# Block sums moved from VectorE to GpSimd in a one-core decoder layer

## The chip, the cores and the metric
The kernel runs on one core of a Trainium2 chip. The metric is the time of one execution on the device in microseconds (us). The kernel before took 449.89 us, the median of 3 runs (449.35 to 450.27).

The core has a matrix engine (TensorE, PE in the profile, with its weight loads as PEld), a vector engine (VectorE, DVE), an activation engine (ScalarE, ACT), a general engine (GpSimd, POOL), and SyncE (SP), which issues the transfers. Each works through a queue of its own in order and waits on semaphores for the others. SBUF is the working memory of all of them; PSUM receives what the matrix engine sums.

## The reference, cut to what matters
One decoder layer over 256 tokens of width 1024. The input is normalised and multiplied by one wide weight, whose columns feed a recurrent branch, a causal attention, a cross-attention over 256 memory tokens, and three gates. A gated sum of the three branches goes through an output projection, and a gated feed-forward block of width 3072 follows. All of it is float32.

```python
h = rms_norm(x, mix_norm_gain[l])
proj = h @ w_in[l]
xa, ga, qm, km, vm, qx, g_logits = jnp.split(proj, splits, axis=-1)
...
branch_out = jnp.einsum("bsnw,nwd->bsnd", ys, w_branch[l])
gates = jax.nn.sigmoid(g_logits)          # three gates, 1024 columns each
merged = jnp.sum(gates * branch_out, axis=2)
x = x + merged @ w_out[l]
...
x = x + (jax.nn.gelu(g) * (h @ w_ffn_up[l])) @ w_ffn_down[l]
```

## The kernel before
**Precision.** Every operand of a product is split in two: ScalarE copies it to a rounded high part, VectorE subtracts that from the operand and keeps the low part. A product is three matmuls: high by high, high by low, low by high.

**Weights.** They arrive in units of 128 x 2048 elements (1 MB). `dma_next` (L138) loads a unit into one of three `wraw` buffers, `split_next` (L173) makes `whi` on ScalarE (L189) and `wlo` on VectorE (L190), three buffers each, and `ahead` (L205), called after each unit's matmuls, keeps the loads four units and the splits two units ahead.

**The first gate as seven products.** The first gate's weight, 1024 rows by 1024 columns, is not multiplied as four plain blocks. It is cut in 2 x 2 blocks B11, B12, B21, B22, and x in 2 x 2 blocks too (two halves of the tokens, two halves of the columns). Four sums S1 to S4 of the blocks of x (L715 to L728) and four sums T1 to T4 of the blocks of the weight stand in for the missing eighth product, in the manner of Strassen and Winograd; `product` (L779) multiplies one block of 128 tokens x 512 by one of 512 x 512, in 12 matmuls.

**Sums of x.** L718 adds the high and low parts of the normalised x again into two tiles `xg` of 128 x 1024. L721 to L724 make S1 and S2 (in `sa`) and S3 and S4 (in `sb`), 128 x 512 each. L727 and L728 split `sa` and `sb` into `sh` and `sl`, two slots at a time.

**Sums of weights.** `add2` (L153) adds two units half by half, 128 x 1024 each. `block_t1` (L157) loads B12 into two tiles and writes T1 = B11 + B12 over B11's buffer, once B11 is split. `block_t2` (L164) loads B22 into the buffer with the tag `sc`, which the cross-attention's probabilities `px` used before, then writes T3 = B12 + B22 over B12, and T2 = T1 + B22 into two new tiles. T4 = T2 + B21 goes over T2 (L182). Their order of use is T2, T1, T3, T4.

**Order of work.** The text is traced in its written order; a scheduler then orders each engine's queue, and lets a later instruction go ahead where an earlier one would still wait by its estimate. The tiles named `s4`, among them `xg`, `sa`, `sb`, B12, and the operands of the cross-attention, share 15 buffers of 128 x 1024. Around the change the written order is: scores of the last heads of the cross-attention (`x_qk`), softmax (`x_norm`, L663), the first half of the third gate's unit with the split of B11 and T1 behind it, transposes of the probabilities and their splits (`x_pt`, L671 to L674), the sums of x, the products with the values (`x_pv`, L682 to L684), the second half of the third gate, then the first block product, branch 1, and the block product of S2 with T2 (L800 to L804).

Of the kernel before, what the change touches and what calls it, by code (L numbers as in the profile page):

```python
# [8 lines left out]
F32 = mybir.dt.float32  # L9
F32R = mybir.dt.float32r  # L10
AF = mybir.ActivationFunctionType
OP = mybir.AluOpType
# [95 lines left out]
def hybrid_trunk(ctx: ExitStack, tc: tile.TileContext, ws, xw, xv, xn, mt, mn, pp, lw, fg, out):  # L108
    nc = tc.nc
    V, A, T, G = nc.vector, nc.scalar, nc.tensor, nc.gpsimd  # L110
# [16 lines left out]
    def a8(nm):  # L127
        t = a8p.tile([128, KC, S], F32R, name=nm, tag="a8")
        return t
# [4 lines left out]
    raw, hi, lo = {}, {}, {}  # L134
# [12 lines left out]
    blk = {}  # L147
    HW = UW // 2

    def halves(t):  # L150
        return [t[:, :HW], t[:, HW:]]

    def add2(o, a, b):  # L153
        for x, y, z in zip(o, a, b):
            V.tensor_add(x, y, z)

    def block_t1(b11):  # L157
        blk["B12"] = [s4("b12", sh=(128, HW)) for _ in range(2)]
        for t, c in zip(blk["B12"], (0, HW)):
            nc.sync.dma_start(t, ws[NU - 2, :, c:c + HW])  # L160
        blk["T1"] = halves(raw[b11])
        add2(blk["T1"], blk["T1"], blk["B12"])

    def block_t2():  # L164
        b22 = ip.tile([128, UW], F32, name="b22", tag="sc", bufs=1)
        nc.sync.dma_start(b22, ws[NU - 1])
        blk["B22"] = halves(b22)
        blk["T3"] = blk["B12"]
        add2(blk["T3"], blk["B12"], blk["B22"])
        blk["T2"] = [s4("t2", sh=(128, HW)) for _ in range(2)]  # L170
        add2(blk["T2"], blk["T1"], blk["B22"])

    def split_next(parts=1):  # L173
        i = st["spl"]
        u = STEPS[i]
        h = wp.tile([128, UW], F32R, name="whi")
        l = wp.tile([128, UW], F32R, name="wlo")
        if u == "T2":
            block_t2()
        elif u == "T4":  # L180
            blk["T4"] = blk["T2"]
            add2(blk["T4"], blk["T2"], halves(raw[i0["B21"]]))  # L182
        if isinstance(u, str):
            src = list(zip(blk[u], halves(h), halves(l)))
        else:
            w = UW // parts
            src = [[t[:, p * w:(p + 1) * w] for t in (raw[u], h, l)] for p in range(parts)]
        for r, hh, ll in src:
            A.copy(hh, r)  # L189
            V.tensor_sub(ll, r, hh.bitcast(F32))  # L190
        hi[i], lo[i] = h, l
        if u == i0["B11"]:
            block_t1(u)
        st["spl"] += 1

    T2S = STEPS.index("T2")
    i0 = {"B11": STEPS[T2S - 2], "B21": STEPS[STEPS.index("B22") - 2]}
# [7 lines left out]
    def ahead():  # L205
        u = st["u"] - 1
        n = max(x for x in STEPS[:min(u + LA_D, NS - 1) + 1] if not isinstance(x, str))
        while st["dma"] <= n:
            dma_next()
        while st["spl"] <= min(u + LA_S, NS - 1):  # L210
            split_next()
# [75 lines left out]
    for k in range(KC):  # L287
        t = ip.tile([128, 1024], F32, name="xw", tag="s4", bufs=15)
# [24 lines left out]
    def s4(nm, dt=F32, sh=(128, 4, S)):  # L313
        t = ip.tile(list(sh), dt, name=nm, tag="s4", bufs=15)
        return t
# [13 lines left out]
    xh, xl = a8("xh"), a8("xl")  # L329
# [3 lines left out]
    for k in range(KC):  # L333
# [7 lines left out]
        else:  # L341
            A.activation(xh[:, k, :], xk, AF.Copy, scale=par("g1", k))
        V.scalar_tensor_tensor(xl[:, k, :], xk, par("g1", k), xh[:, k, :].bitcast(F32),
                               op0=OP.mult, op1=OP.subtract)
# [3 lines left out]
        for j, (a, b) in enumerate(((h, xh), (h, xl), (l, xh))):  # L348
            for m in range(4):
                c = slice(512 * (k % 4) + m * 128, 512 * (k % 4) + m * 128 + 128)  # L350
                T.matmul(b0[m][:, :S], lhsT=a[:, c], rhs=b[:, k, :], start=(k == 0 and j == 0),  # L351
                         stop=(k == KC - 1 and j == 2))
    st["spl"] = st["u"] = 2
    split_next(2)
    split_next(2)
    ahead()
    sq = s4("sq", sh=(128, D))
# [47 lines left out]
    e, z, y, q, n8 = [cst.tile([128, 4], F32, name=f"sp{i}") for i in range(5)]  # L405
# [271 lines left out]
    def x_pv(h):  # L677
        b = ac_bank()
        for m in range(2):
            hs_ = slice(h * 128, (h + 1) * 128)  # L680
            ph, pl = pxs[h]
            mm3(b[:, :S], mvh[:, m, hs_], mvl[:, m, hs_], ph[:, m, :], pl[:, m, :], m == 0, m == 1)  # L682
        A.copy(ych[:, h, :], b[:, :S])
        V.tensor_sub(ycl[:, h, :], b[:, :S], ych[:, h, :].bitcast(F32))  # L684
# [6 lines left out]
    for g in range(2):  # L691
        d = slice(2 * g, 2 * g + 2)
# [9 lines left out]
    for t in range(2):  # L702
        A.activation(mvh[:, t, :], vb[t], AF.Copy, scale=rsm[:, t:t + 1])
        V.scalar_tensor_tensor(mvl[:, t, :], vb[t], rsm[:, t:t + 1], mvh[:, t, :].bitcast(F32),
                               op0=OP.mult, op1=OP.subtract)
# [8 lines left out]
    sh, sl = a8p.tile([128, 4, 4, 128], F32R, name="sh", tag="a8"), a8p.tile([128, 4, 4, 128], F32R, name="sl", tag="a8")  # L714
    xg = [s4("xg"), s4("xg")]  # L715
    for kh in range(2):
        k = slice(4 * kh, 4 * kh + 4)
        V.tensor_add(xg[kh], xh[:, k, :].bitcast(F32), xl[:, k, :].bitcast(F32))  # L718
    a11, a21, a12, a22 = [xg[i][:, :, t * 128:(t + 1) * 128] for i in range(2) for t in range(2)]
    sa, sb = s4("sa", sh=(128, 2, 4, 128)), s4("sb", sh=(128, 2, 4, 128))  # L720
    V.tensor_sub(sa[:, 0], a22, a21)  # L721
    V.scalar_tensor_tensor(sa[:, 1], a11, -1.0, sa[:, 0], op0=OP.mult, op1=OP.subtract)
    V.tensor_sub(sb[:, 0], a11, a21)
    V.scalar_tensor_tensor(sb[:, 1], a12, -1.0, sa[:, 1], op0=OP.mult, op1=OP.subtract)  # L724
    for i, t in ((0, sa), (1, sb)):
        d = slice(2 * i, 2 * i + 2)
        A.copy(sh[:, d], t)  # L727
        V.tensor_sub(sl[:, d], t, sh[:, d].bitcast(F32))  # L728
    x_pv(0)
    x_pv(1)  # L730
    x_pt(3)
# [118 lines left out]
    for i in range(2):  # L850
        t = a8p.tile([128, 4, 2, S], F32R, name="h2", tag="a8")
# [73 lines left out]
    def ffn_gate(f, bk):  # L925
        g = gp[f % 3]
        t = fp.tile([128, 2, S], F32, name="tcv", bufs=3)
        t2 = join(bk)
        V.tensor_mul(g[:, :, 2:], t2, rb2x)
        for m in range(2):  # L930
            b = 2 * f + m
            A.activation(t[:, m, :], g[:, m, 2:], AF.Identity, scale=par("fw", 48 + b), bias=par("fb", b))
            V.scalar_tensor_tensor(t[:, m, :], g[:, m, 1:1 + S], par("fw", 24 + b), t[:, m, :], op0=OP.mult, op1=OP.add)
            V.scalar_tensor_tensor(t[:, m, :], g[:, m, 0:S], par("fw", b), t[:, m, :], op0=OP.mult, op1=OP.add)  # L934
        A.activation(t, t, AF.Gelu_apprx_tanh)  # L935
        return t
# [45 lines left out]
    for f in range(1, 13):  # L982
        if f < 12:
# [4 lines left out]
            t = ffn_gate(f, gbk)  # L988
# [14 lines left out]
    for i, (t, c0, c1) in enumerate(FIN):  # L1003
        o = dz[i - 3][:, :256] if i > 2 else db[t][c0 // 512][:, c0 % 512:c0 % 512 + c1 - c0]
        V.scalar_tensor_tensor(yf[:, t, c0:c1], o, rs2[:, t:t + 1], (yf if i > 2 else x2)[:, t, c0:c1], op0=OP.mult,
                               op1=OP.add)
        x = slice(t, t + 1)
# [20 lines left out]
        for c in (512, 768):  # L1028
            V.scalar_tensor_tensor(yg[:, t, c:c + 256], yf[:, t, c:c + 256], r3[:, x], fgb[:, c:c + 256], op0=OP.mult,
                                   op1=OP.mult)  # L1030
# [75 lines left out]
```

## Time and profile before
| | us | share of the span |
|---|---|---|
| profiled execution, device time | 449.81 | |
| its span | 448.0 | 100% |
| PE, 2486 matmuls | 438.4 | 98% |
| PEld | 383.2 | 86% |
| DVE, 458 instructions | 345.5 | 77% |
| ACT, 374 instructions | 274.9 | 61% |
| POOL, 21 instructions | 18.9 | 4% |

Busy time is time in which an engine had an instruction running; the ends of matmuls are modelled and they overlap, so that the step from one start to the next tells more than a duration. A row of the timeline gives the start, the time, the engine, the line of the code, the operation, output and inputs with their shapes, the count of merged instructions, and in brackets the idle time before it with what ended that. PEclk is the matrix engine's granted clock as a share of 2.4 GHz.

### The profile page before, as it was taken

The numbers are of one execution on the slowest core, as the hardware profiler recorded it, in microseconds if no ns is written. First come the engines' busy times: TensorE is split into PE (matmuls) and PEld (weight loads), VectorE is DVE, ScalarE is ACT, GpSimd is POOL, SyncE is SP. The second block draws the span as 40 slices with busy tenths as digits, with TensorE's granted clock in tenths as the row PEclk, the third lists the DMA queues.
The fourth block names the chain that finished last, engine by engine and source line by source line (L and its number), as shares of the span: only waits on it lengthen the run. The fifth ranks groups of instructions, "written<-read, shape, count | busy, mean of one in ns | idle before, by whom it ended". The sixth has DMA issues, their size and how long they took to land.

```text
span 448.0 us, 6270 instructions
## 1 busy us (share of the span) xinstructions
PE 438.4 (98%) x2486; PEld 383.2 (86%) x2486; DVE 345.5 (77%) x458; ACT 274.9 (61%) x374; POOL 18.9 (4%) x21
## 2 busy tenths in 40 slices
PE   9999999999999899999999999999999999999994
PEld 9999879998888688888888888888888888888883
DVE  6679799999699997848767798766676677677664
ACT  6675989986655547554347676554554554554543
POOL 2000200130000000000001200000000000000011
PEclk9999999999999899999999999999999999999999
DMA  8975753556525356265445555545545555545102
GB/s 300 412 283 189 282 197 140 189 191 223 191 93 189 98 192 274 94 228 201 168 169 199 199 203 189 189 181 190 195 178 200 196 178 208 193 162 222 53 0 94
DMA packets 13852, 84.38 MB, mean 188 GB/s; under 512 B 1792, under 2 KB 2304, under 8 KB 4608
## 3 DMA queue, kind: packets, MB, share of 16 engines
q1 hardware_dynamic: 13392, 82.95, 50.3%
q0 software_dynamic: 144, 0.52, 0.5%
q10 hardware_dynamic: 288, 0.52, 0.3%
q8 instruction: 19, 0.31, 0.3%
q14 instruction: 9, 0.07, 0.0%
HBM read 82.94 MB, written 1.05 MB: 187 GB/s over the span
## 4 chain that ended last, share of the span: by engine, by line
PE 91%; DVE 6%; ACT 1%; issue 1%; DVEq 0%; ACTq 0%
PE mm L234 18%; PE mm L237 9%; PE ac L976 5%; PE ac L977 5%; PE ac L978 5%; PE ac L247 4%; PE ac L248 4%; PE ac L249 4%; PE mm L785 4%; PE mm L247 3%; PE mm L248 3%; PE mm L249 3%; PE mm L219 3%; PE mm L220 3%; PE mm L221 3%; PE mm L351 3%
## 5 line engine op out<-in xcount | busy, mean ns | idle before, releaser
L190 DVE TENSOR_TENSOR wlo<-wraw,whi 128x2048 fp32r<-128x2048 f32 (+1 forms) x74 | 164.1, 2220 | 68.8 <-ACT whi L189 68.5
L189 ACT CAST whi<-wraw 128x2048 fp32r<-128x2048 f32 (+1 forms) x74 | 135.9, 1839 | 79.4 <-PE mm L234 29.8
L234 PE MATMUL mm<-h,whi 128*128 128x512 f32 x352 | 88.8, 392 | 0.0
L234 PEld LDWEIGHTS mm<-h,whi 128*128 128x128 f32 x352 | 63.7, 189 | 11.6
L237 PEld LDWEIGHTS mm<-h,wlo 128*128 128x128 f32 x352 | 48.6, 190 | 3.8
L237 PE MATMUL mm<-h,wlo 128*128 128x256 f32 x352 | 49.7, 282 | 0.0
L976 PE MATMUL ac<-whi,ah 128*128 128x512 f32 x92 | 35.9, 392 | 0.0
L977 PE MATMUL ac<-wlo,ah 128*128 128x512 f32 x92 | 35.8, 391 | 0.0
L978 PE MATMUL ac<-whi,al 128*128 128x512 f32 x92 | 35.7, 390 | 0.0
L921 ACT COPY join<-mm 128x256 f32<-128x256 f32 x44 | 15.9, 364 | 18.6 <-PE mm L237 18.5
L935 ACT ACTIVATE tcv<-tcv 128x512 f32<-128x512 f32 x12 | 7.6, 632 | 27.0 <-DVE tcv L934 27.0
L219 PE MATMUL mm<-xh,whi 128*128 128x256 f32 x80 | 22.8, 284 | 0.0
L220 PE MATMUL mm<-xl,whi 128*128 128x256 f32 x80 | 22.6, 283 | 0.0
L221 PE MATMUL mm<-xh,wlo 128*128 128x256 f32 x80 | 22.6, 283 | 0.0
L978 PEld LDWEIGHTS ac<-whi,al 128*128 128x128 f32 x92 | 17.3, 188 | 3.8 <-DVE al L945 0.2
L976 PEld LDWEIGHTS ac<-whi,ah 128*128 128x128 f32 x92 | 17.3, 188 | 3.5 <-ACT ah L944 0.3
L977 PEld LDWEIGHTS ac<-wlo,ah 128*128 128x128 f32 x92 | 17.3, 188 | 3.2
L247 PE MATMUL mm<-whi,xh 128*128 128x512 f32 x48 | 18.9, 395 | 0.0
L249 PE MATMUL mm<-whi,xl 128*128 128x512 f32 x48 | 18.8, 392 | 0.0
L248 PE MATMUL mm<-wlo,xh 128*128 128x512 f32 x48 | 18.7, 391 | 0.0
L922 DVE TENSOR_TENSOR join<-mm,join 128x256 f32<-128x256 f32 x44 | 17.4, 417 | 0.3 <-ACT join L921 0.3
L219 PEld LDWEIGHTS mm<-xh,whi 128*128 128x128 f32 x80 | 15.4, 192 | 0.3 <-issue 0.3
(332 smaller groups left out, 914.5 us busy)
## 6 DMA issues: line engine op xcount, KB each, us to landing
wraw<-in_ws_dram SPq DMA_DIRECT2D x68, 1024.0 KB, 4.8
xw<-in_xv_dram SPq DMA_DIRECT2D x6, 388.0 KB, 6.4
wraw<-in_ws_dram SPq DMA_DIRECT2D x4, 512.0 KB, 9.9
x<-in_xn_dram SPq DMA_DIRECT2D x1, 1024.0 KB, 13.8
mnat<-in_mn_dram SPq DMA_DIRECT2D x1, 1024.0 KB, 5.5
mr<-in_mt_dram SPq DMA_DIRECT2D x1, 1024.0 KB, 4.8
b<-in_ws_dram SPq DMA_DIRECT2D x2, 512.0 KB, 6.8
b<-in_ws_dram SPq DMA_DIRECT2D x1, 1024.0 KB, 4.7
```

Source lines behind the costliest of these rows:

```text
L189: A.copy(hh, r)
L190: V.tensor_sub(ll, r, hh.bitcast(F32))
L219: T.matmul(banks[m], lhsT=wh[:, k, c], rhs=rh[:, k, :], start=(k == 0), stop=False)
L220: T.matmul(banks[m], lhsT=wh[:, k, c], rhs=rl[:, k, :], start=False, stop=False)
L234: T.matmul(banks[m], lhsT=wh[:, k, c], rhs=hc[k // 4][:, k % 4].rearrange("p a t -> p (a t)"), start=(k == 0), stop=False)
L237: T.matmul(banks[m][:, :S], lhsT=wl[:, k, c], rhs=hc[k // 4][:, k % 4, 0, :], start=False, stop=(k == KC - 1))
L247: T.matmul(banks[t], lhsT=ah[:, k0 + k, s], rhs=wh[:, k, :], start=first and k == 0, stop=False)
L248: T.matmul(banks[t], lhsT=ah[:, k0 + k, s], rhs=wl[:, k, :], start=False, stop=False)
L249: T.matmul(banks[t], lhsT=al[:, k0 + k, s], rhs=wh[:, k, :], start=False, stop=last and k == 3)
L976: T.matmul(o, lhsT=ah[:, k, s], rhs=wh[:, k, cs], start=first, stop=False)
L977: T.matmul(o, lhsT=ah[:, k, s], rhs=wl[:, k, cs], start=False, stop=False)
L978: T.matmul(o, lhsT=al[:, k, s], rhs=wh[:, k, cs], start=False, stop=end)
```

## The change
GpSimd makes the two sums `xg`, the four sums S1 to S4, and T3 and T4; T1 and T2 stay on VectorE. Since L722 made minus the sum in its slot, that slot now holds the sum without the sign, and its split multiplies by -1 on the way; S4 is a plain subtraction of it. The split of the four sums goes slot by slot, as four copies on ScalarE and four subtractions on VectorE.

```diff
-    def add2(o, a, b):
+    def add2(o, a, b, eng=V):
         for x, y, z in zip(o, a, b):
-            V.tensor_add(x, y, z)
+            eng.tensor_add(x, y, z)
...
-        add2(blk["T3"], blk["B12"], blk["B22"])
+        add2(blk["T3"], blk["B12"], blk["B22"], G)
         blk["T2"] = [s4("t2", sh=(128, HW)) for _ in range(2)]
         add2(blk["T2"], blk["T1"], blk["B22"])
...
-            add2(blk["T4"], blk["T2"], halves(raw[i0["B21"]]))
+            add2(blk["T4"], blk["T2"], halves(raw[i0["B21"]]), G)
...
-        V.tensor_add(xg[kh], xh[:, k, :].bitcast(F32), xl[:, k, :].bitcast(F32))
+        G.tensor_add(xg[kh], xh[:, k, :].bitcast(F32), xl[:, k, :].bitcast(F32))
...
-    V.tensor_sub(sa[:, 0], a22, a21)
-    V.scalar_tensor_tensor(sa[:, 1], a11, -1.0, sa[:, 0], op0=OP.mult, op1=OP.subtract)
-    V.tensor_sub(sb[:, 0], a11, a21)
-    V.scalar_tensor_tensor(sb[:, 1], a12, -1.0, sa[:, 1], op0=OP.mult, op1=OP.subtract)
-    for i, t in ((0, sa), (1, sb)):
-        d = slice(2 * i, 2 * i + 2)
-        A.copy(sh[:, d], t)
-        V.tensor_sub(sl[:, d], t, sh[:, d].bitcast(F32))
+    G.tensor_sub(sa[:, 0], a22, a21)
+    G.tensor_add(sa[:, 1], a11, sa[:, 0])
+    G.tensor_sub(sb[:, 0], a11, a21)
+    G.tensor_sub(sb[:, 1], sa[:, 1], a12)
+    for i, (t, f) in enumerate(((sa[:, 0], 1.0), (sa[:, 1], -1.0), (sb[:, 0], 1.0), (sb[:, 1], 1.0))):
+        A.activation(sh[:, i], t, AF.Copy, scale=f)
+        V.scalar_tensor_tensor(sl[:, i], t, f, sh[:, i].bitcast(F32), op0=OP.mult, op1=OP.subtract)
```

## Rows read from the trace of the kernel before
**Rows 1.** The page's first part: busy time, share of the span, instructions.
```profile
PE 438.4 (98%) x2486; PEld 383.2 (86%) x2486; DVE 345.5 (77%) x458; ACT 274.9 (61%) x374; POOL 18.9 (4%) x21
```
**Rows 2.** Waits of PE: for whom, us in total, times, longest.
```profile
PE ac L247 <- ACT whi L189: 1.3, 1, 1.3
PE mm L785 <- DVE t L155: 0.9, 1, 0.9
```
**Rows 3.** Timeline of PE around those two waits.
```profile
145.22 0.39 PE L247 MATMUL ac<-whi,ybh 128*128 128x512 f32 x1
...
146.36 0.39 PE L249 MATMUL ac<-whi,ybl 128*128 128x512 f32 x1
...
149.42 0.80 PE L247 MATMUL ac<-whi,ych 128*128 128x512 f32 x1 [1.30 <-ACT whi L189]
...
155.87 0.39 PE L249 MATMUL ac<-whi,ycl 128*128 128x512 f32 x1
```
**Rows 4.** Busy time by stretch: PE, PEld, DVE, ACT, POOL, then PEclk and DMA.
```profile
138.00:146.00 8.00, 8.00 (x40) 6.69 (x39) 8.00 (x12) 5.51 (x8) 0.00 (x0) 1.00 0.36 150
...
150.00:152.00 2.00, 2.00 (x6) 1.62 (x5) 2.00 (x1) 2.00 (x3) 0.00 (x0) 0.50 0.00 0
```
**Rows 5.** One group of VectorE by shape: busy us, mean ns, idle before.
```profile
L155 DVE TENSOR_TENSOR b<-b,b 128x1024 f32<-128x1024 f32 x2 | 2.4, 1221 | 0.0
```
**Rows 6.** Groups of GpSimd by shape.
```profile
L1017 POOL TENSOR_TENSOR yg<-yf,fgb 128x512 f32<-128x512 f32 x2 | 2.6, 1296 | 187.4 <-DVE yf L1005 187.4
L564 POOL TENSOR_TENSOR ig<-ig,xc 128x1024 f32<-128x1024 f32 x1 | 2.4, 2394 | 48.8 <-ACT ig L451 48.8
```
**Rows 7.** Timelines of GpSimd and VectorE where both worked.
```profile
83.19 1.89 POOL L563 TENSOR_TENSOR rg<-av 128x1024 f32<-128x1024 f32 x1 [28.72 <-ACT av L562]
95.60 4.29 POOL L620 TENSOR_TENSOR ga_t<-ga_t,th 128x1024 f32<-128x1024 f32 x1 [10.52 <-ACT whi L189]
...
83.55 3.00 DVE L549 SCALAR_TENSOR_TENSOR ml<-mr,ppa,mh 128x256 fp32r<-128x256 f32 x4
...
95.38 2.26 DVE L190 TENSOR_TENSOR wlo<-wraw,whi 128x2048 fp32r<-128x2048 f32 x1
97.56 0.68 DVE L594 TENSOR_TENSOR ev<-mm,rb 128x512 f32<-128x512 f32 x1
...
98.50 3.54 DVE L190 TENSOR_TENSOR wlo<-wraw,whi 128x2048 fp32r<-128x2048 f32 x1
```
**Rows 8.** Line L549: instructions, least, median and longest ns.
```profile
L549 DVE SCALAR_TENSOR_TENSOR ml<-mr,ppa,mh x8: 470/480/1817, 77.0 to 86.1; 128x256 fp32r<-128x256 f32 x8
```
**Rows 9.** Timeline of VectorE, 122 to 148 us, in order.
```profile
124.33 2.28 DVE L190 TENSOR_TENSOR wlo<-wraw,whi 128x2048 fp32r<-128x2048 f32 x1
126.53 0.17 DVE L661 RECIPROCAL rsx<-smx 128x4 f32<-128x4 f32 x1
126.62 1.20 DVE L718 TENSOR_TENSOR xg<-xh,xl 128x1024 f32<-128x1024 f32 x1
127.73 2.36 DVE L155 TENSOR_TENSOR wraw<-wraw,b 128x1024 f32<-128x1024 f32 x2
130.00 1.29 DVE L663 TENSOR_TENSOR px<-px,rsx 128x512 f32<-128x512 f32 x2
131.20 1.88 DVE L674 TENSOR_TENSOR pl<-ac,ph 128x512 fp32r<-128x512 f32 x3
...
145.20 2.36 DVE L155 TENSOR_TENSOR t<-wraw,b 128x1024 f32<-128x1024 f32 x2
```
**Rows 10.** Timeline of PE: last scores, and the first product with `pl`.
```profile
122.60 0.28 PE L436 MATMUL ac<-mkh,qxl 128*128 128x256 f32 x1
...
132.17 0.28 PE L435 MATMUL ac<-pl,mvh 128*128 128x256 f32 x1
```
**Rows 11.** Tile `b`: the load of B22, issued at; then the page's transfers, us to landing.
```profile
L166 SPq DMA_DIRECT2D b<-in_ws_dram x1: 328/328/328, 134.2 to 134.2; - x1
...
b<-in_ws_dram SPq DMA_DIRECT2D x1, 1024.0 KB, 4.7
```

## The prediction
> **What bounds the kernel now.** I read the page's busy times first: TensorE is busy for 98% of the span, VectorE for 77%, GpSimd for 4% [rows 1]. So TensorE sets the time, and another engine matters only where it lets TensorE wait or costs it its clock. The view of waits for TensorE answers where: apart from one wait at the very start there are two, 0.9 us for the sum T2 on VectorE and 1.3 us for a high part on ScalarE [rows 2]. Both lie at the first use of T2, in the product with S2, and the timeline shows their whole price. A usual step from one matmul's start to the next is 0.23 us (145.22 to 146.36 in five steps). From 146.36 to 155.87 there are 23 steps, which would take 23 x 0.228 = 5.24 us; they take 9.51 [rows 3]. The stretch costs 4.27 us: 2.60 of waiting (146.36 to 149.42 less two steps), and 1.67 because the granted clock falls to 0.50 of 2.4 GHz, its lower level of 1.2, after the waits [rows 4]. That is all that this change can win: 449.81 - 4.27 = 445.5 us.
>
> Why is T2 late? VectorE's timeline: B22 is requested at 134.2 and takes 4.7 us to land, so it is there at 138.9 [rows 11], but T2's sum starts at 145.20 [rows 9], with no idle time on VectorE in between (8.00 of 8.00 us in 138 to 146 [rows 4]). VectorE's queue is the cause.
>
> **What leaves VectorE.** Ahead of T2: two sums `xg` at 1.13 a step (1.20 less the overlap with the next), four sums of S at 0.60 (the step of a 128x512 operation with two inputs, as in the two of L663, 1.29 together), and T3, two at 1.13 [rows 5, 9]. That is 2.26 + 2.40 + 2.26 = 6.9 us. Added: the split of S in four of 0.60 in place of two of 1.13, 0.1 us. T4 later saves another 2.3 us, where TensorE waits for nothing. ScalarE's copies become four for two; it has 2.5 us free in 8 there [rows 4], so I cost that at nothing, and if that cover were gone, at their starts, a few tenths. The sign costs nothing, since the copy and the subtraction carry a factor either way.
>
> **What GpSimd takes for it.** A 128x1024 product with two inputs took 2.39 us while VectorE did next to nothing, a 128x512 one 1.30 [rows 6]. The work is 2 x 2.39 for `xg`, 4 x 1.30 for S, 2 x 2.39 for T3 and as much for T4: 19.5 us on an engine that is busy for 18.9 in the whole span [rows 1]. Bounds of a 1024 one: 1.89 with one tensor as both inputs, and 4.29 beside VectorE [rows 7].
>
> **What the two do to each other.** At 83.19 GpSimd starts an operation of 1.89 us, until 85.08. VectorE starts a 256-wide one at 83.55 whose usual time is 0.48; it takes 1.82, until 85.37 [rows 7, 8]. At 95.60 GpSimd starts while VectorE is in a low-part subtraction until 97.64; it takes 4.29, that is 1.9 longer than alone. VectorE's next, which reads PSUM, keeps its 0.68 beside it, and the subtraction after, from 98.50, takes 3.54 against 2.28 [rows 7, 9]. So an operation of VectorE with two inputs in SBUF and one of GpSimd don't run together: the second waits. Operations with a PSUM source pass. From the row, VectorE reads again 0.19 us before GpSimd's recorded end (85.37 - 0.48 = 84.89), so GpSimd shuts it out for 2.20 or 1.11 us a time. The Trainium skill has the same exclusion in "SBUF — State Buffer", Who interferes with whom, but blocks the second for the whole instruction; by it the six operations below would cost 6 x 0.19 = 1.1 us more, and the result would be 453.2. The measured row decides, and I use it.
>
> No row shows what happens when both have work queued: whether GpSimd gets in after each operation of VectorE (they alternate) or VectorE goes on until something else lets GpSimd in. The nearest row is 98.50, where the waiting engine started as soon as the other was done; no instruction of the same engine was let in front of it. I take alternation and keep the other for a rival.
>
> **Where it falls on the path.** `xg`, `sa` and `sb` need four of the 15 `s4` buffers. By the written order these are all held until the last scores have read `qxh`, `qxl`, `mkh`, `mkl` at 122.60 + 0.28 [rows 10], so GpSimd starts at about 122.9, when VectorE's queue is at its fullest. The queue by its rows [rows 9], with GpSimd's turns:
> - `xg` 0 from 122.9 to 125.3; the low part of B11, due at 124.33, starts at 125.1 and yields at 127.3.
> - `xg` 1 shuts VectorE out until 129.5.
> - Then the two `px` (0.60 each) and the two halves of T1 (1.13 each) stand before the first `pl`, in whichever order, with one of the four sums of S before each but the first: 0.09 for the reciprocal (126.53 to 126.62) + 1.20 + 2.26 + 3 x 1.11 = 6.9, until 136.4.
> - The first `pl` starts at 136.4 in place of 131.20 [rows 9], 5.2 us late, though 1.1 us of `xg` is gone from before it.
>
> TensorE's first matmul with `pl` starts at 132.17, and that `pl` was ready at 131.88 [rows 9, 10]: 0.3 us of slack, in a queue worked in order. So TensorE waits 4.9 us there. Behind that matmul stand the rest of the third gate, the first block product and all that follows. The clock falls after this wait as it did after 2.6 us of waiting; I take the same 1.7 us [rows 3, 4]. Everything on TensorE is then 6.6 us later, so T2's use moves from 146.6 to about 153. B22's buffer comes free later too: 134.2 + 4.9 + 4.7 = 143.8. T3 and T2 then alternate, 2 x 2.20 + 2 x 1.13 = 6.7, until 150.5. The old wait is gone or nearly so: -4.27.
>
> Sum: 4.9 + 1.7 - 4.27 = +2.3. Against the execution that was profiled, 449.81 (a span of 448.0 and 1.8 around it; the median of the runs is 0.08 higher): **452.1 us**.
>
> S itself is made in time: the last sum ends under the `pl` operations at about 138, before VectorE comes to its split. T4 shares the port with low parts at 164 to 171, where VectorE has gaps; it holds B21's buffer up to 2.4 us longer, and loads run four units ahead: nothing, at most 2.4.
>
> **Rivals.**
> - *VectorE keeps the port.* GpSimd only gets `xg` 1 in behind the low part of B11 (the reciprocal reads one small input), and the sums of S run under the `pl` operations. Then `pl` starts at 129.5 + 0.1 + 3.46 = 133.1, 1.9 late, and TensorE waits 1.6. T2 is then early enough. 1.6 - 4.27 = -2.7, or -1.0 if the clock falls too: 447.1 to 448.8, say 448.0. For it: back-to-back operations of VectorE overlap by 0.09 us at their ends [rows 9]. Against: at 97.5 GpSimd got in at once.
> - *All of it hidden: faster by the whole stall.* The scheduler writes TensorE's queue anew. If it puts the second half of the third gate, 24 matmuls x 0.228 = 5.5 us, before the first `pl`, the 5.2 us are covered and T2's wait goes: 445.5. It decides once `pl` is late in the scheduler's own estimate as well. Against: before, it placed that matmul 0.3 us behind its input, and with `xg` off VectorE it may move it forward.
> - *The relief doesn't reach T2.* T3 on GpSimd starts when B22 lands, as T2 does, and goes first; each half of T2 waits 2.2 us. With the delay of 122 to 138 small, T2 ends where it did: 449 to 451.
> - *Both stalls.* `pl` late and T2 late again by another 2 to 4 us: 454 to 457.
>
> **How the numbers follow.** Alternation as summed 0.40, both stalls 0.10, VectorE keeps the port 0.22, all hidden 0.18, no relief 0.10. A measurement of this kernel tells about 0.2%, 0.9 us, from no change. All hidden (0.18) and most of the second case (0.20 of 0.22) are faster by more; alternation and both stalls are slower by more but for 0.04, no relief by 0.04 of its 0.10. That makes faster 0.38, same 0.12, slower 0.50. Signs of both kinds are likely, so the range spans them: from 446.0, which leaves out the best of the hidden case, to 456.0, which leaves out the worst of both stalls. The likeliest case alone reaches from 450.5 to 454.5.
>
> **What would show it.** Right: low parts and `px` stretched by 1 to 2 us between 124 and 137, GpSimd's operations with waits of VectorE's length in them, a wait of TensorE of 3 to 6 us for `pl` near 130 to 137 with a granted clock of 0.5 behind it, and none at T2. Wrong: the first `pl` before 133, or GpSimd's operations bunched where VectorE reads PSUM, or TensorE's queue with the third gate's second half ahead of the first `pl`; or `xg` on GpSimd before 122.

## The result and the profile after

The changed kernel takes 452.52 us (median of 10 runs, 450.65 to 453.21) against 449.35 for the kernel before on the same chip: a ratio of 1.006, 95% interval 1.0042 to 1.0078. It is slower by some 3 us, near the 452.1 that was forecast. The ten runs fall in two groups, four at 450.65 to 451.33 with a mean granted clock of 0.996 over the span and six at 452.30 to 453.21 with 0.992 or 0.993. The wait that was meant to go is gone; two new ones are there, and neither is the one that the forecast named.

The execution that was profiled took 450.65 us, the shortest of the ten, with a span of 448.6. A second profile of the same kernel (the first experiment) is of an execution of 453.7 and a span of 451.6. Both are used below. Outside the span lie 2.0 to 2.15 us in every run of this kernel, against 1.7 to 1.85 in the runs of the kernel before: about 0.3 us of the loss is not in the profile at all, and no run here shows its cause.

The busy times of the kernel after, to stand beside [rows 1]; then the waits of TensorE (PE), beside [rows 2], without the one in the first microseconds that both kernels have:

```profile
PE 436.8 (97%) x2486; PEld 381.0 (85%) x2486; DVE 350.6 (78%) x450; ACT 275.6 (61%) x376; POOL 45.5 (10%) x31
```

```profile
PE ac L671 <- DVE px L663: 2.9, 1, 2.9
PE ac L248 <- DVE wlo L190: 1.3, 2, 0.8
```

Ten sums left VectorE (DVE), 2.26 + 2.40 + 2.26 + 2.26 = 9.2 us of work by the prices of the forecast, and its busy time rose by 5.1. The busy time of an engine that is shut out counts on, so this row already says that its other instructions became longer. GpSimd (POOL) works 26.6 us more for what was estimated at 19.5. The timeline of GpSimd says where:

```profile
107.22 6.80 POOL L718 TENSOR_TENSOR xg<-xh,xl 128x1024 f32<-128x1024 f32 x2 [7.81 <-DVE yal L632]
122.39 1.29 POOL L721 TENSOR_TENSOR sa<-xg 128x512 f32<-128x512 f32 x1 [8.37 <-PE ac L436]
123.65 1.30 POOL L723 TENSOR_TENSOR sb<-xg 128x512 f32<-128x512 f32 x1
124.90 3.40 POOL L722 TENSOR_TENSOR sa<-xg,sa 128x512 f32<-128x512 f32 x1
128.38 2.12 POOL L724 TENSOR_TENSOR sb<-sa,xg 128x512 f32<-128x512 f32 x1
141.21 5.75 POOL L155 TENSOR_TENSOR b<-b,b 128x1024 f32<-128x1024 f32 x2 [10.71 <-DMA b<-in_ws_dram]
161.15 6.04 POOL L155 TENSOR_TENSOR t<-t,wraw 128x1024 f32<-128x1024 f32 x2 [14.18 <-DMA wraw<-in_ws_dram]
```

`xg` runs at 107 to 114, released by a low part on VectorE, some 15 us before the point that the forecast gave for it. The four sums of S do start when the last scores have been read (122.39), as forecast. VectorE's timeline in the same stretches, to stand beside [rows 9]:

```profile
111.70 2.88 DVE L596 TENSOR_TENSOR mkl<-ev,mkh 128x512 fp32r<-128x512 f32 x1
...
123.15 0.56 DVE L655 TENSOR_SCALAR mxx<-mxx 128x2 f32<-128x2 f32 x1
...
124.29 0.68 DVE L655 TENSOR_SCALAR mxx<-mxx 128x2 f32<-128x2 f32 x1
124.88 2.28 DVE L190 TENSOR_TENSOR wlo<-wraw,whi 128x2048 fp32r<-128x2048 f32 x1
...
127.19 4.39 DVE L155 TENSOR_TENSOR wraw<-wraw,b 128x1024 f32<-128x1024 f32 x2
131.51 1.28 DVE L663 TENSOR_TENSOR px<-px,rsx 128x512 f32<-128x512 f32 x2
...
133.47 1.89 DVE L674 TENSOR_TENSOR pl<-ac,ph 128x512 fp32r<-128x512 f32 x3
...
141.49 3.21 DVE L155 TENSOR_TENSOR t<-wraw,b 128x1024 f32<-128x1024 f32 x1
...
161.51 6.76 DVE L190 TENSOR_TENSOR wlo<-b,whi 128x1024 fp32r<-128x1024 f32 x2
```

Read the two timelines against each other. GpSimd's third sum starts at 124.90 behind VectorE's low part (124.88 to 127.16) and takes 3.40. VectorE goes on with T1 at 127.19, and its two halves take 4.39 (2.19 and 2.28 one by one) where they took 2.36: one half waits for the sum that ends at 128.30, and before the other GpSimd puts in its last sum (128.38 to 130.50). So GpSimd got in between two instructions that VectorE had back to back. At T3 and T2 it is the same, a half of each in turn: a half of T2 takes 3.21 where it took 1.22. At T4, two halves of a low part take 6.76 in place of 2.35.

What TensorE sees of it, in its timeline (in brackets the idle time before an instruction and what ended it):

```profile
129.02 0.40 PE L249 MATMUL mm<-whi,xl 128*128 128x512 f32 x1
132.33 0.63 PE L671 MATMUL ac<-ident,px 128*128 128x128 f32 x4 [2.92 <-DVE px L663]
...
149.45 0.39 PE L784 MATMUL mm<-whi,sh 128*128 128x512 f32 x1
...
153.32 0.50 PE L248 MATMUL ac<-wlo,ych 128*128 128x512 f32 x1 [0.77 <-DVE wlo L190]
170.53 0.50 PE L248 MATMUL ac<-wlo,xh 128*128 128x512 f32 x1 [0.56 <-DVE wlo L190]
```

S2, the first use of T2, starts at 149.45 without a wait, and the two windows [rows 4] that lay at 1.00 and 0.50 before are both at 1.00. The 2.9 us stand at the transposes of the third head's `px`. In the kernel before these start at 130.92 without a wait, with eight of the gate's matmuls between them and the transposes ahead of them; after, there are three. So the scheduler moved them forward by 1.1 us (five steps of 0.228) to a point whose input comes 1.5 us later (`px` starts at 131.51 for 130.00 in [rows 9]), while all of TensorE ran 0.5 earlier (its last scores at 122.1 for 122.6 in [rows 10]). 1.1 + 1.5 + 0.5 is 3.1, less the 0.1 to 0.2 of slack that there was. The 0.77 at 153.32 is branch 2's low part, now behind a stretched T2; the 0.56 at 170.53 is a low part behind those that T4 stretched.

What all this is worth is best read between two fixed points of TensorE's timeline, since the start of the program varies by up to 1.2 us between the executions below (last scores at 122.09 to 123.25): from the start of the last scores to the start of the last product with S2. Behind it every kernel here takes the same, 262.0 to 262.1 us to the end of the span.

| kernel, profiled execution | last scores | last product with S2 | between |
|---|---|---|---|
| before | 122.60 | 186.02 | 63.4 |
| after, first profile | 122.09 | 186.53 | 64.4 |
| after, second profile | 122.56 | 189.62 | 67.1 |
| x_only | 123.23 | 187.03 | 63.8 |
| t_only | 122.50 | 186.83 | 64.3 |
| xg_only | 123.25 | 183.72 | 60.5 |
| no_read | 123.02 | 184.45 | 61.4 |
| s_more | 122.93 | 191.57 | 68.6 |
| inplace | 122.75 | 184.00 | 61.3 |
| xg_t3 | 122.81 | 182.25 | 59.4 |
| t3_late | 122.73 | 183.39 | 60.7 |
| xg_t2 | 122.78 | 184.01 | 61.2 |

For xg_t3 (below) the view of waits lists none in this stretch, so its 59.4 is taken as the work. The old stall is 63.4 - 59.4 = 4.0. The kernel after loses 5.0 in its first profile: 2.92 + 0.77 + 0.56 = 4.25 in the three waits, the rest in steps that are a little long. In its second profile it loses 7.7.

### The profile page after: what moved, and what is told of

The parts are those of the page before. It is cut to its first block, busy times and chain, and to the rows that moved or that the text cites. A ratio compares the mean times of both kernels' runs of the same rounds, so it can differ in the third digit from the quotient of the medians.

```text
span 448.6 us, 6284 instructions
## 1 busy us (share of the span) xinstructions
PE 436.8 (97%) x2486; PEld 381.0 (85%) x2486; DVE 350.6 (78%) x450; ACT 275.6 (61%) x376; POOL 45.5 (10%) x31
## 4 chain that ended last, share of the span: by engine, by line
PE 89%; DVE 6%; POOL 2%; issue 2%; ACT 1%; DVEq 0%; POOLq 0%
PE mm L234 18%; PE mm L237 9%; PE ac L975 5%; PE ac L976 5%; PE ac L977 5%; PE mm L247 4%; PE mm L249 4%; PE mm L248 4%; DVE wlo L190 3%; PE ac L248 3%; PE ac L249 3%; PE ac L247 3%; PE mm L219 3%; PE mm L220 3%; PE mm L221 3%; PE mm L351 3%
## 5 line engine op out<-in xcount | busy, mean ns | idle before, releaser
L1016 POOL TENSOR_TENSOR yg<-yf,fgb 128x512 f32<-128x512 f32 x2 | 2.6, 1298 | 187.2 <-DVE yf L1004 187.2
```

## The experiments

Theory A throughout: GpSimd and VectorE take turns where both have work with SBUF inputs, the sums of S do this ahead of `px`, and TensorE's wait there, with what its clock does behind it, is the loss; `xg` costs nothing. The rivals are named in the expectations. "Before" is the kernel before on the same chip in the same set; the sets of experiments ran on three chips, so times of different sets are compared by their distance from it.

**after_again**: the changed kernel once more, unedited, with the profile of another execution.

> The changed kernel once more, beside the experiments, for a second profile. In the first profile TensorE waits 2.9 us for px of the third head and its granted clock does not fall; the mean granted clock of the runs comes in two values, 0.996 (451 us) and 0.993 (453 us). Theory A (the sums of S shut VectorE out while it makes T1, so px is late; the clock falls after that wait in some executions): 451 to 453, and a profile at 0.993 shows a stretch at 0.5 right behind the wait for px, worth 1.5 to 2 us. Rival B (the two levels come from somewhere else in the span): the stretch at 0.5 lies elsewhere, or the 2 us are spread.

Measured: 453.33 us (452.07 to 453.74) against 449.92, ratio 1.007 (1.0055 to 1.0085). That is a little above the 453 expected. The same wait of 2.9 us is there, and behind it, in the view of windows (the first seven columns are the stretch, its length and the five engines' busy times, then the granted clock):

```profile
132.00:134.00 2.00, 1.20 (x5) 1.24 (x6) 1.92 (x5) 2.00 (x3) 0.00 (x0) 0.51 0.02 4
134.00:136.00 2.00, 2.00 (x6) 1.54 (x6) 2.00 (x4) 0.88 (x2) 0.00 (x0) 0.50 0.00 0
136.00:138.00 2.00, 2.00 (x11) 1.97 (x10) 1.83 (x4) 0.37 (x1) 0.00 (x0) 0.50 0.00 0
138.00:140.00 2.00, 2.00 (x11) 1.82 (x11) 0.76 (x3) 1.09 (x3) 0.00 (x0) 0.78 0.00 0
```

In the first profile the clock stood at 1.00 in these windows, and the stretch of the table is 2.7 us shorter, with waits that differ by 0.1 in all. So the clock does fall behind this wait, in some executions, and the stretch is up to 2.7 us longer then. The granted clock over the whole span agrees: 0.996 and 0.992 or 0.993 in the two groups of the first ten runs, 451.0 and 452.8 us in the mean, so 1.9 apart. In these six it agrees by and large: 0.996 at 452.07, 0.990 at the three from 453.57 up, 0.992 at 453.09, but also at 452.31.

**x_only** and **t_only** split the change in two: the first has the sums of x on GpSimd and the weight sums on VectorE, the second the reverse (and the kernel before's split of S).

```diff
# x_only, from after
-        add2(blk["T3"], blk["B12"], blk["B22"], G)
+        add2(blk["T3"], blk["B12"], blk["B22"])
...
-            add2(blk["T4"], blk["T2"], halves(raw[i0["B21"]]), G)
+            add2(blk["T4"], blk["T2"], halves(raw[i0["B21"]]))
```

> xg and S on GpSimd, all four weight sums on VectorE. Theory A (the loss is made by the S sums between 122 and 131 us, the T3 sums only slow T2 without reaching TensorE): the wait for px stays at 2.5 to 3.2 us, 450.5 to 453, as the full change or up to 1 us better. Rival C (the T3 sums, which alternate with T2 on VectorE, are what costs): the time falls below the kernel before, 446 to 448.

```diff
# t_only, from before (add2 takes its engine as in the whole change)
...
-        add2(blk["T3"], blk["B12"], blk["B22"])
+        add2(blk["T3"], blk["B12"], blk["B22"], G)
...
-            add2(blk["T4"], blk["T2"], halves(raw[i0["B21"]]))
+            add2(blk["T4"], blk["T2"], halves(raw[i0["B21"]]), G)
```

> T3 and T4 on GpSimd, xg and S on VectorE as before. Theory A: px is not late and there is no wait for it; T2 gains 2.3 us in VectorE's queue and loses up to 4.4 to GpSimd's T3, so the wait at T2 stays or grows a little: 449 to 451.5. Rival C: 451.5 to 453, slower than before by the whole loss of the change.

x_only: 450.71 (450.08 to 451.29), 1.0022 (1.0012 to 1.0033). Its one wait is the 2.9 us for `px`, and T1 is stretched as in the whole change. Behind the wait the granted clock is down to 0.50 in the window from 134 to 136, and the stretch of the table loses 4.4 us, 1.5 more than the wait:

```profile
PE ac L671 <- DVE px L663: 2.9, 1, 2.9
```

```profile
128.33 4.39 DVE L155 TENSOR_TENSOR wraw<-wraw,b 128x1024 f32<-128x1024 f32 x2
```

t_only: 450.99 (450.21 to 451.13), 1.0018 (1.001 to 1.0027). No wait for `px`; others, worth 3.9 us, in place of the old two (2.2), with the clock at 1.00 in the windows from 130 to 152:

```profile
PE ac L248 <- DVE wlo L190: 1.7, 2, 1.4
PE ac L435 <- DVE pl L674: 1.2, 1, 1.2
...
PE ac L247 <- ACT whi L189: 1.0, 1, 1.0
```

Its T3 starts on GpSimd at 139.04, when the split of S is still in VectorE's queue, and that split takes the blow, with the last `pl` behind it:

```profile
139.30 3.22 DVE L728 TENSOR_TENSOR sl<-sa,sh 128x1024 fp32r<-128x1024 f32 x1
142.45 0.68 DVE L674 TENSOR_TENSOR pl<-ac,ph 128x512 fp32r<-128x512 f32 x1
```

So neither half wins: each removes work ahead of T2 and gives as much or more back at another place. Theory A is too narrow: x_only is 2.6 us below after_again in the same set, where it allowed 1, so the weight sums cost too. Their two waits, 1.4 us in after_again, are part of that, and so are the clock's fall, which is longer there, and 0.3 us outside the span, where x_only and t_only have 1.7 to 1.85 us like the kernel before. No run parts the rest.

**xg_only** moves the two `xg` sums alone.

```diff
# from before
-        V.tensor_add(xg[kh], xh[:, k, :].bitcast(F32), xl[:, k, :].bitcast(F32))
+        G.tensor_add(xg[kh], xh[:, k, :].bitcast(F32), xl[:, k, :].bitcast(F32))
```

> Only the two sums xg on GpSimd, where they ran from 107 to 114 us in the profile of the changed kernel, ahead of the crowded stretch. Theory A: nothing of GpSimd is left in 122 to 131, VectorE's queue is 2.3 us shorter there, the wait at T2 shrinks from 2.6 us to under 1 and the clock may hold: 446 to 448, faster than both kernels. Rival D (TensorE's new order alone, with the transposes of the third head moved ahead, makes the loss): a wait for px of 1 us or more is there with xg_only too, and it is not faster, 449 to 451.

Measured: 447.15 (446.52 to 447.52), 0.9938 (0.9926 to 0.995): faster than both kernels. TensorE's waits are down to 0.3 us; T1 keeps its 2.35, and the first T2 sum starts at 143.78 for 145.20:

```profile
PE ac L248 <- DVE wlo L190: 0.3, 1, 0.3
```

```profile
112.83 2.88 DVE L596 TENSOR_TENSOR mkl<-ev,mkh 128x512 fp32r<-128x512 f32 x1
...
127.94 2.35 DVE L155 TENSOR_TENSOR wraw<-wraw,b 128x1024 f32<-128x1024 f32 x2
...
143.78 2.35 DVE L155 TENSOR_TENSOR t<-wraw,b 128x1024 f32<-128x1024 f32 x2
```

`xg` shuts VectorE out as well: `mkl` takes 2.88, where it takes 0.69 before. No wait of TensorE appears there. The same interference costs 0 at one place and 3 us at another.

**no_read** keeps the whole change and puts GpSimd's four reading sums of S out of the way: it writes a constant into S in their place, so S is not computed.

```diff
# from after
-    G.tensor_sub(sa[:, 0], a22, a21)
+    G.memset(sa[:, 0], 0.5)      # and so the other three
```

> The changed kernel with the four sums of S replaced by four fills of the same tiles by GpSimd, which read nothing (so S holds a constant, and the first gate's values are not the reference's). The queues of VectorE and TensorE stay as in the changed kernel but for one split that moves 0.6 us. Theory A (GpSimd's reads shut VectorE out): T1 takes 2.3 us in place of 4.4, px comes 2 us earlier, the wait for px falls from 2.9 us to between 0.3 and 1, the clock holds, T3 still alternates with T2: 448 to 449.5. Rival D (TensorE's new order makes the wait, whatever GpSimd does): 2 us or more of it stay, 451 to 453.

Measured: 448.69 (448.46 to 449.4) against 449.41, 0.9981 (0.9972 to 0.999). The `px` wait is gone, and T1 has its usual time:

```profile
PE ac L248 <- DVE wlo L190: 1.4, 2, 0.9
```

```profile
127.74 2.35 DVE L155 TENSOR_TENSOR wraw<-wraw,b 128x1024 f32<-128x1024 f32 x2
```

The transposes of the third head still start 0.2 us behind their place, too little for the view of waits. The expectation took TensorE's queue to stay as in the changed kernel. It did not quite: ahead of these transposes stand five of the gate's matmuls, as in xg_only, xg_t3 and xg_t2, where after, x_only, s_more and inplace, in which GpSimd makes S, have three, and before, t_only and t3_late eight. Two steps of 0.228 are 0.5 us. The rest comes from `px`, which starts 7.0 us behind the last scores (130.01 and 123.02) in place of 9.4 (131.51 and 122.09): 2.4 us earlier. Of that, T1's two turns are 2.0 and the steps behind the two `mxx` 0.9, less 0.6 for a split that VectorE does ahead of T1 here. Together with the order it is the 2.9 by which the delay shrank, so rival D, the order alone, is worth 0.5 of it. What is left are the 1.4 us of the weight sums.

The run does not show what writes alone would do to T1, since the fills were over by then. The last of them ran beside the low part of B11, which kept its 2.28:

```profile
124.67 0.52 POOL L724 MEMSET sb<- 128x512 f32 x1
```

```profile
124.87 2.28 DVE L190 TENSOR_TENSOR wlo<-wraw,whi 128x2048 fp32r<-128x2048 f32 x1
```

**s_more** is the opposite: the last sum of S is made three times.

```diff
# from after, behind the last sum of S
+    G.tensor_sub(sb[:, 1], sa[:, 1], a12)
+    G.tensor_sub(sb[:, 1], sa[:, 1], a12)
```

> The changed kernel with the last sum of S made three times over, two more operations of 1.3 us on GpSimd. If the engines take turns (theory A), one of the two falls between T1 and the third head's px, the other between the two px: the wait for px grows by one turn, from 2.9 to between 3.9 and 4.2, and the time by 1 to 1.5, to 453.5 to 455. If VectorE goes first once it has work queued (the second case of the prediction): no more than 0.3 us. If GpSimd goes first: 2.4 us more.

Measured: 455.46 (454.95 to 456.14), 1.0133 (1.0114 to 1.0153). The wait, GpSimd and VectorE:

```profile
PE ac L671 <- DVE px L663: 4.0, 1, 4.0
```

```profile
129.24 2.13 POOL L724 TENSOR_TENSOR sb<-sa,xg 128x512 f32<-128x512 f32 x1
131.44 2.12 POOL L725 TENSOR_TENSOR sb<-sa,xg 128x512 f32<-128x512 f32 x1
133.64 1.60 POOL L726 TENSOR_TENSOR sb<-sa,xg 128x512 f32<-128x512 f32 x1
```

```profile
128.04 4.41 DVE L155 TENSOR_TENSOR wraw<-wraw,b 128x1024 f32<-128x1024 f32 x2
132.37 3.42 DVE L663 TENSOR_TENSOR px<-px,rsx 128x512 f32<-128x512 f32 x2
```

Here the alternation is plain: GpSimd's sums start 2.20 us apart, a half of T1 or one `px` in each gap. One more turn ahead of the third head's `px` makes the wait 1.1 us longer, the price of a turn in the forecast. Had VectorE kept the port, the added sums would have run later and the wait stayed at 2.9. The stretch of the table is 1.5 us longer than after_again's (68.6 for 67.1), which the turn and 0.5 us of growth in the other waits cover. The time rose by more: it is 6.05 us above its own before, after_again 3.41, so 2.6 more, and 455.46 lies above the 453.5 to 455 that theory A gave. Where the last microsecond stands is open.

**inplace** tries to save the idea: S is written over the blocks of `xg`, so that no buffer holds the sums back until the scores have been read. Weight sums on VectorE.

```diff
# from x_only
-    sa, sb = s4("sa", sh=(128, 2, 4, 128)), s4("sb", sh=(128, 2, 4, 128))
-    G.tensor_sub(sa[:, 0], a22, a21)
...
+    G.tensor_sub(a22, a22, a21)
+    G.tensor_sub(a21, a11, a21)
+    G.tensor_add(a11, a11, a22)
+    G.tensor_sub(a12, a11, a12)
```

> xg and S on GpSimd as in the changed kernel, the weight sums on VectorE, and S written over the blocks in xg, so that its sums need no buffers of their own and need not wait for the last scores at 122 us: GpSimd should do all six right behind each other, from about 107 to 121 us, ahead of T1. Theory A: T1 takes 2.3 us, no wait for px over 0.3, VectorE's queue 4.6 us shorter ahead of T2, no wait at T2: 445.5 to 447, up to 1.5 us below the kernel with only xg on GpSimd. Rival E (the crowd from 107 to 121 has no room for more than xg, the low parts of mk late for the scores): a wait for mkl or px of 1 us or more, 447.5 to 450.

Measured: 448.1 (447.73 to 448.27), 0.9969 (0.9957 to 0.998): faster than before, slower than xg_only. The sums ran from 114.77 to 122.51, well clear of T1. A wait of 1.7 us for `px` is still there, though, with another origin: the scaling of the scores' maxima, an instruction of 128x2 elements with one input, takes 0.15 in xg_only and this here:

```profile
116.95 0.84 DVE L655 TENSOR_SCALAR mxx<-mxx 128x2 f32<-128x2 f32 x1
...
119.91 1.25 DVE L655 TENSOR_SCALAR mxx<-mxx 128x2 f32<-128x2 f32 x1
```

The two stretches push all that stands behind them in VectorE's queue by 0.7 + 1.1 = 1.8 us, the exponentials' input too, and `px` with it; the transposes are again moved forward by five matmuls. It is the same instruction that takes 0.56 and 0.68 in the kernel after. The case that the expectation set against theory A came true in its size, not by its way.

**xg_t3, t3_late, xg_t2.** With the two `xg` sums gone, is it VectorE's order at T2 that is left? T3's sum stands ahead of T2's though T3 is used later. t3_late puts it behind, and moves nothing to GpSimd; xg_t3 does both; xg_t2 has xg_only's move and only swaps the two sums in place.

```diff
# t3_late, from before; xg_t3 has the xg line of xg_only as well
     def block_t2():
...
-        blk["T3"] = blk["B12"]
-        add2(blk["T3"], blk["B12"], blk["B22"])
...
         if u == "T2":
             block_t2()
+        elif u == "T3":
+            blk["T3"] = blk["B12"]
+            add2(blk["T3"], blk["B12"], blk["B22"])
```

> The kernel before with the two sums of x on GpSimd (as in xg_only) and with T3's sum written at T3's own split, behind T2's. No sum runs on GpSimd while VectorE has two-input work queued, and T2's sum no longer stands behind T3's, which took 2 x 1.22 us or more. Theory A (what is left in xg_only is VectorE's queue order at T2 and branch 2): the 0.3 us wait of L248 goes, T2 comes 2.4 us earlier, 445.5 to 446.8 us, 0.3 to 1.5 below xg_only's 447.15. Theory B (after the two sums left, TensorE is full there and the order no longer matters): 446.9 to 447.4. Theory C (branch 2's low part or T3 becomes the late one): a wait of L247, L248 or of T3's product shows, 447.5 or more.

> The kernel before with nothing on GpSimd and T3's sum written at T3's own split, behind T2's: one move in VectorE's queue, meant for the same two waits. Theory A (the old 0.9 us at T2 and 1.3 us at branch 2, with the fall of the clock behind them, are made by the order of VectorE's queue): T2's sum starts 2.4 us earlier, its wait goes, most of branch 2's goes, 446.5 to 448.5 us. Theory C (branch 2's low part is late whatever the order, as VectorE has the same work up to it): the 1.3 us stay and the clock falls there, 448.8 to 449.8.

> As xg_only, with T2's sum written before T3's in the same place of the program: T3's sum stays ahead of branch 2's low part. Theory A: T2 earlier by 2.4 us, the wait of L248 (0.3 us) stays as it was, since VectorE has the same work ahead of branch 2's low part, 446.6 to 447.3 us. Theory B (the order does not matter any more): the same as xg_only, 446.9 to 447.4. If xg_t3 gains and xg_t2 does not, it is T3's place ahead of branch 2 that decides, not T2's.

xg_t3: 446.0 (445.9 to 446.13) against 449.93, 0.9912 (0.9899 to 0.9926), the fastest of all and below both kernels. After the first 9 us the view of waits lists none for TensorE. T2 starts at 141.07, and only one half of T3 is made ahead of branch 2's low part, which is the first of the three at 147.97:

```profile
141.07 2.35 DVE L155 TENSOR_TENSOR t<-wraw,b 128x1024 f32<-128x1024 f32 x2
143.34 1.21 DVE L155 TENSOR_TENSOR b<-b,b 128x1024 f32<-128x1024 f32 x1
144.47 1.21 DVE L191 TENSOR_TENSOR wlo<-t,whi 128x1024 fp32r<-128x1024 f32 x1
...
147.97 4.55 DVE L191 TENSOR_TENSOR wlo<-wraw,whi 128x2048 fp32r<-128x2048 f32 x3
```

t3_late: 447.23 (446.87 to 447.49), 0.9939 (0.9927 to 0.9952): as much as xg_only with nothing on GpSimd. One wait is left, at branch 2, now for a low part:

```profile
PE ac L249 <- DVE wlo L191: 1.3, 1, 1.3
```

It is as long as the old wait at branch 2, but the clock stays at 1.00 behind it. So most of the 2.7 us that t3_late wins over before in the table are T2's wait of 0.9 and the fall of the clock behind the two old waits, 1.67 by the forecast.

xg_t2: 448.05 (447.79 to 448.11), 0.9958 (0.9944 to 0.997), 0.9 us worse than xg_only, which no theory expected. T2 starts at 141.04 for 143.78, 2.3 us earlier from the last scores, but the scheduler now places a product of another unit where its high part on ScalarE isn't ready:

```profile
PE ac L247 <- ACT whi L189: 1.5, 1, 1.5
```

An earlier T2 was thus worth nothing by itself here; what counted was the whole order up to branch 2.

## Why the prediction came out as it did

- *The price of the old stall, 4.27 us.* Held. It is gone in the kernel after, and xg_t3, which loses it and gains no other, is 4.0 us shorter in the stretch and stands at 446.0, half a microsecond from the 445.5 that the forecast gave as the floor. The part of it that is clock varies between executions: in the three sets the kernel before takes 448.65 to 449.70 where its mean granted clock is 0.998, and 450.31 to 450.67 at 0.991 or 0.992.
- *The exclusion of GpSimd and VectorE, and alternation where both have work queued.* Held, by T1's 4.39, by the turns of s_more and by its 4.0 us. The rival "VectorE keeps the port" falls by the same rows. The forecast limited the exclusion to VectorE's operations with two inputs in SBUF; `mxx` shows one with a single small input, which made `px` 0.9 us later in the kernel after than in no_read. (The six operations by which the forecast got 453.2 are five in its own queue: two of `xg` and three of S.)
- *Where `xg` runs.* Wrong. The forecast said that all buffers are held until 122.9. `xg`'s were free at 107, released by a low part (L632), and the two sums ran some 15 us earlier, hidden: one of the signs of being wrong that the forecast had listed. Only `sa` and `sb` had to wait for the scores. Two turns of 2.20 us thus fell out of the queue ahead of `pl`; the forecast had them as its largest item.
- *TensorE waits for the first `pl`, 4.9 us.* Wrong in place and size: 2.9 us for `px`, the operation ahead of it in the same chain. The forecast took TensorE's queue as it was, with `pl` as the first thing that could be late, and allowed in a rival that the scheduler would move work forward to cover it. Against the kernel before, the scheduler moved the transposes forward instead, by five matmuls, 1.1 us of the 2.9.
- *The clock behind it, 1.7 us.* Right in kind; the size is not one number: nothing in one profiled execution, most of the 2.7 us by which the stretch is longer in the other, and 1.9 between the two groups of runs.
- *B22 later, T2 without a wait.* Held: B22 released T3 at 141.2 (143.8 forecast, after a longer wait), T3 and T2 alternate, S2 starts without waiting. Branch 2's low part right behind, which the forecast did not follow, is late by 0.77.
- *T4 costs nothing, at most 2.4.* It costs a wait of 0.56 us at 170.53.

In sum the forecast had +4.9 + 1.7 - 4.27 = +2.3. Measured in the stretch it is 4.25 in waits, 0.75 in long steps, nothing or 2.7 for the clock, and -4.0: +1.0 or +3.7; about 0.3 outside the span comes on top. That the time came out close is in part luck: the wait in the third gate is 2.0 us shorter than forecast (2.92 for 4.9), and the two late low parts and the long steps, which the forecast put at nothing, are 2.1. The clock's 1.7 lies between the nothing and the 2.7 of the two profiles, and the median falls in the group of six; in the group of four it would have been near 451. That the clock alone makes the difference between the two executions rests on the windows; no experiment here sets it.

## What to carry to other kernels

A second engine that reads the same memory was not spare capacity here: price a move to GpSimd by what VectorE has queued at the very time when the moved work becomes free to start, which is set by buffers as much as by data. Moved work was worth its price where VectorE's victims had slack (`xg` at 107, 2.8 us better), and harmful in front of a chain that TensorE reads next (the sums of S at 122). Look for an order first: one sum written a little later won as much as the best move.

## What the hardware did that was not expected

- A TENSOR_SCALAR of 128x2 elements with a single SBUF input was shut out like the large ones: 0.56 to 1.25 us for a usual 0.15. The Trainium skill ("SBUF — State Buffer", Who interferes with whom) names this kind among those that can enter a mode with two ports and then contend with GpSimd; these rows agree.
- VectorE did not hold its place by having its next instruction ready: GpSimd got in between back-to-back instructions each time (2.20 us from start to start of 128x512 sums, in s_more, against 1.26 at 122.39 to 123.65 in the kernel after, where of VectorE's such work only a small `mxx` stood in between).
- A fill by GpSimd, which writes without reading, did no such thing: beside the last of four in no_read the low part of B11 kept its 2.28. By the same section of the Trainium skill an operation of VectorE with two SBUF inputs contends only with GpSimd's reads; this row agrees. The `mxx` just ahead of it is recorded with 0.41 for 0.15, but the next instruction starts 0.07 us after its start, as it does without a fill.
- The same wait of 2.9 us was followed by a granted clock of 0.50 for some 7 us in the second profile of the kernel after, for some 3 us in x_only, and by 1.00 in the first profile; what decides between them stays open.
